# Experts of a decoder block: TensorE's instructions in the order of the program

## The chip, the cores and the metric

One Trainium2 chip, one of its cores. The core has five engines that run side by side and meet at semaphores: TensorE (PE in the profile, its weight loads as PEld), VectorE (DVE), ScalarE (ACT), GpSimd (POOL) and SyncE (SP), which here only issues DMA. Sixteen DMA engines move data between the memory (HBM) and the core's SBUF. The metric is the device time of one execution, in microseconds (us), as the median of several runs.

## The reference

One decoder block for 512 tokens of width 2048, all in float32. The first part is attention and retention with their projections; the change does not touch it. The second part is a mixture of 32 experts:

```python
g_sel = argmax(softmax(h @ w_rg + b_rg))             # one of 4 groups per token
top_p, top_i = top_k(softmax(e_logits of g_sel), 2)   # two of its 8 experts
weights = p_group * top_p / sum(top_p)
for e in range(32):                                   # D_MODEL 2048, D_EXPERT 512
    x_e = tokens that picked e
    y_e = (silu(x_e @ w1[e]) * (x_e @ w3[e])) @ w2[e]
out = rmsnorm(h + sum over picks of weight * y_e)
```

Each expert has w1, w3 (2048 x 512) and w2 (512 x 2048), 12.58 MB together; 32 experts have 402.7 MB. The 512 tokens make 1024 picks, 32 per expert in the mean.

## The kernel before

The kernel is written in a framework in which a scheduler decides, engine by engine, the order in which the traced instructions stand, from its own estimates of their durations. A function can take an engine out of its hands (`manual_schedule`): that engine's instructions then stand in the order in which the program wrote them. In the kernel before only SP is out of its hands, from the start on.

For each expert e the program traces these steps:

- **prep** (lines 714 to 755). GpSimd compares ranks and builds a selection matrix S (128 x 4 x 128, line 718). Four small matmuls (`ax`, line 723) give the inverse norms `rs` and, by way of three VectorE steps, the row numbers `idx` of the scatter. The gather (line 733) is 192 bf16 matmuls that pick up to 64 tokens out of the three bf16 parts of h, turned, in two halves g = 0 and 1 of 96 matmuls each, each in its own PSUM tile `gp`; VectorE scales each half into `xs` (line 736).
- **gemm1** (lines 762 to 780). `ab` = xs times w1 and w3: 16 steps, each of two float32 matmuls side by side in the two column halves of the array (line 759 in `halves_mm`). The two halves g of it use the weight tiles (0, 2) and (1, 3) of the expert. Then, in the same function, ScalarE copies `ab` out (line 772), TensorE turns it (`tr`, line 775), ScalarE takes the silu `sg` (line 777), VectorE multiplies to `gs` (line 779).
- **gemm2** (lines 785 to 815). `y` = gs times w2 in two halves q = 0 and 1; both halves read both of the expert's w2 tiles (4, 5). ScalarE copies half 0 and VectorE half 1 into `ysb`, and GpSimd issues an indirect DMA (line 813, the scatter) that writes the rows to `ybuf` in HBM. There is one `ysb`.

The outer loop (line 893 on) traces gemm1(e), prep(e + 1), gemm2(e - 1). The `y` and `ax` tiles share two PSUM buffers (`psY`).

Weights come in 192 loads of 2048 KB, six per expert, each into one of 8 buffers that are used in turn (`buffer`, `pieces_of`). SP issues them in the program's order: four for gemm1(e), then two for gemm2(e - 1). A load waits until the buffer that it takes, that of eight loads before, has been read for the last time, and the loads behind it in SP's queue wait with it. Near the end two of the eight buffers are kept for `fw` and `ys`. Behind the experts, `combine` (line 926) loads `ybuf` again, adds it to h, normalises and writes the output.

Of the kernel before, what the change touches and what calls it, by code (L numbers as in the profile page):

```python
# [11 lines left out]
F32 = mybir.dt.float32  # L12
F32R = mybir.dt.float32r
# [8 lines left out]
P = 128  # L22
D = 2048
# [6 lines left out]
NE = 32  # L30
# [96 lines left out]
def hybrid_block(ctx, tc, a, out):  # L127
    nc = tc.nc
# [303 lines left out]
    for j in range(KT):  # L432
        for n in range(2):
            acc = proj_T(f"g{n}", j)
            g = work("gs")
# [29 lines left out]
    with pool("mtmp", 2, reuse_waits="tile") as mt:  # L465
        for j in range(KT):
            hi, lo = unit("br", j, after=done[3] if j == 1 else None)
            gs, bs = [], []
            for n in range(2):
                g = mt.tile([P, T], F32, name=f"g{n}")  # L470
# [155 lines left out]
    scC = ExitStack()  # L626
# [28 lines left out]
    _, oh1 = first_max(LE, NT, NG, EPG)  # L655
    gm, ohg = first_max(L[:, :, :NG], NT, NG)
    nc.vector.scalar_tensor_tensor(LE2, oh1, NEG, LE, op0=OP.mult, op1=OP.add)
    _, oh2 = first_max(LE2, NT, NG, EPG)
# [43 lines left out]
    def buffer(shape=(P, 4096), dtype=F32, keep=False):  # L702

        pl, tag = next(x for x in loads if x[1] not in kept)
        if keep:
            kept.add(tag)
        return pl.tile(list(shape), dtype, name="wraw", tag=tag)

    gathering = []
    rowbase = rp[0].tile([P, 1], F32, name="rowbase")  # L710
    nc.gpsimd.memset(rowbase[:SLOTS], 8192.0)
# [2 lines left out]
    def prep(rsel, is2, eng, late=False):  # L714

        S = cp.tile([P, NT, P], BF, name="S")
        for t in range(NT):
            i = eng.tensor_scalar(S[:, t], slot1.rearrange("p a b -> p (a b)"), rsel[:, t:t + 1], None,  # L718
                                  op0=OP.is_equal)
        gathering.append(i.ins)  # L720
        ax = psY.tile([P, 40], F32, name="ax", tag="y")
        for t in range(NT):
            nc.tensor.matmul(ax, S[:, t], aux[:, t], start=(t == 0), stop=(t == NT - 1))  # L723
        rs = cp.tile([P, 1], F32, name="rs", bufs=3)
        nc.vector.reduce_sum(rs, ax[:, 0:3], axis=AX.X)
        xs = cp.tile([P, KT, SLOTS], F32, name="xs")
        for g in range(2):
            ks = slice(8 * g, 8 * g + 8)
            gp = psG.tile([P, 8, SLOTS], F32, name="gp")
            for d in range(8):  # L730
                for t in range(NT):
                    for i in range(3):
                        nc.tensor.matmul(gp[:, d], h3[i][:, t, (8 * g + d) * P:(8 * g + d + 1) * P],  # L733
                                         S[:, t, :SLOTS], start=(t == 0 and i == 0),
                                         stop=(t == NT - 1 and i == 2))
            nc.vector.tensor_mul(xs[:, ks], gp, b3(nfw[:, ks, None], 8, SLOTS))  # L736
        if late:
            ws = psY.tile([P, 3], F32, name="ws", tag="y")
            for t in range(NT):
                nc.tensor.matmul(ws, S[:, t], auxw[:, t], start=(t == 0), stop=(t == NT - 1))  # L740
            wsl = cp.tile([P, 1], F32, name="wsl", bufs=1)
            nc.vector.reduce_sum(wsl, ws, axis=AX.X)
            sp = psR.tile([P, NT, P], F32, name="tr")
            for t in range(NT):
                nc.tensor.matmul(sp[:, t], S[:, t], idb, start=True, stop=True)
            sT = cp.tile([P, NT, P], F32R, name="sT", bufs=1)
            nc.scalar.copy(sT, sp)
            return xs, rs, (wsl, sT)
        ix = cp.tile([P, 1], F32, name="ix", bufs=3)
        idx = cp.tile([P, 1], I32, name="idx", bufs=3)  # L750
        nc.vector.reduce_sum(ix, ax[:, 3:6], axis=AX.X)
        nc.vector.tensor_add(ix, ix, rowbase)
        nc.vector.scalar_tensor_tensor(idx, is2(ax[:, 8:40]), 2.0, ix, op0=OP.mult, op1=OP.add)
        return xs, rs, idx

    def halves_mm(acc, st, w, first, last):

        for m in range(2):
            nc.tensor.matmul(acc[m * SLOTS:(m + 1) * SLOTS], st, w[m], start=first, stop=last)  # L759

    def gemm1(blk, pieces):

        xs, rs, idx = blk
        acc = psA.tile([P, DE], F32, name="ab")
        for g in range(2):
            w = [next(pieces), next(pieces)]
            for kk in range(8):
                k = 8 * g + kk
                halves_mm(acc, xs[:, k], [w[m][:, kk * DE:(kk + 1) * DE] for m in range(2)],
                          k == 0, k == KT - 1)  # L770
        sb = cp.tile([P, DE], F32, name="ab", bufs=1)
        nc.scalar.activation(sb, acc, AF.Copy, scale=rs)  # L772
        tr = psR.tile([P, 4, P], F32, name="tr")
        for k in range(4):
            nc.tensor.transpose(tr[:, k], sb[:, k * P:(k + 1) * P], ident)
        sg = cp.tile([P, 4, SLOTS], F32, name="sg", bufs=1)
        nc.scalar.activation(sg, tr[:, :, :SLOTS], AF.Silu)
        gs = cp.tile([P, 4, SLOTS], F32, name="gs")
        last_ins.append(nc.vector.tensor_mul(gs, tr[:, :, SLOTS:], sg))
        return gs, idx  # L780

    last_ins = []
    yp = []

    def gemm2(blk, pieces, ys=None):

        gs, idx = blk
        if ys is not None:
            wsl, sT = idx
        else:  # L790
# [27 lines left out]
    def pieces_of(we, part):  # L818

        for q in ((4, 5) if part else (0, 2, 1, 3)):  # L820
            w = buffer()
            nc.sync.dma_start(w, we[q])
            yield w

    def prep_e(e):
        return prep(rank1[:, :, e], lambda c: c[:, e:e + 1], nc.gpsimd if e else nc.vector, e == NE - 1)
# [21 lines left out]
    def spread_fw(fw):  # L848

        for g in range(4):  # L850
            b = psR.tile([P, 4, P], F32, name="tr")
            for k in range(4):
                j = 4 * g + k
                nc.tensor.matmul(b[:, k], ident[:KT, j:j + 1].to_broadcast([KT, P]), fwk, start=True, stop=True)
            nc.scalar.copy(fw[:, g * T:(g + 1) * T], b.rearrange("p a b -> p (a b)"))
# [32 lines left out]
        return wt  # L888

    yp.append(scC.enter_context(pool("yout", 1, reuse_waits="tile")))  # L890
    x0 = prep_e(0)
    prev = None
    for e in range(NE):
        if e == NE - 1:
            fw = buffer((P, D), F32, True)
            ys = buffer((P, D), F32R, True)
            gemm2(prev, pieces_of(a["wM"][e - 1], 1))
            spread_fw(fw)
        cur = gemm1(x0, pieces_of(a["wM"][e], 0))
        if e == 8:  # L900
            with tc.issue_after(last_ins[-1].ins):
                nblk, eid, sta, en, it = extra_blocks()
        if e == 12:
            with tc.issue_after(last_ins[-1].ins):
                wtf = mixing()
        if e + 1 < NE:
            x0 = prep_e(e + 1)
        if 0 < e < NE - 1:
            gemm2(prev, pieces_of(a["wM"][e - 1], 1))
        prev = cur  # L910

    def diagonals():

# [3 lines left out]
        return dgs  # L917

    dgs = diagonals()
    sT = gemm2(prev, pieces_of(a["wM"][NE - 1], 1), ys)  # L920


    yv = ybuf.rearrange("(t p k) d -> t p k d", p=P, k=2)
# [48 lines left out]
    with tc.If(n_extra > 0):  # L972
        with tc.For_i(0, n_extra, 1):
# [11 lines left out]
            rsel, tmp4 = f("rsel", NT), oh1.rearrange("p t g j -> p t (g j)")  # L985
# [11 lines left out]
            ev = nc.values_load(eid[0:1, 0:1], engines=[mybir.EngineType.SP], min_val=0, max_val=NE - 1)  # L997

            we = a["wM"][ds(ev, 1)].rearrange("e q p n -> (e q) p n")
            gemm2(gemm1(prep(rsel, is2, nc.vector), pieces_of(we, 0)), pieces_of(we, 1))  # L1000
        combine(diagonals())
    scC.close()

# [69 lines left out]
```

## Time and profile before

| | us |
|---|---|
| median of 3 runs (2638.57 to 2646.08) | 2644.53 |
| the profiled execution, its own time | 2639.73 |
| its span, first to last instruction | 2637.9 |
| TensorE busy, of the span | 2433.3 |
| projections, attention, routing: up to about | 1440 |
| experts: from the first `ax` to the last `y` | 1442.7 to 2595.6 |
| the end (`combine`) | 2595.6 to 2637.9 |

The profile's page divides the span into 40 equal slices. Other views list the instructions in order of time, what each waited for, or the busy times of all engines in a chosen stretch. A busy PE says that matmuls were in its pipe, not that it ran at its best; PEclk is the share of full clock (2.4 GHz) that the chip granted.

### The profile page before, as it was taken

To read this page: it belongs to the slowest core of one execution; us is meant where nothing else is said; L and a number is where in the kernel's file an instruction comes from. 1 tells how busy PE (TensorE), PEld (TensorE's weight loads), DVE (VectorE), ACT (ScalarE), POOL (GpSimd) and SP (SyncE) were. 2 spreads that over 40 slices of the span, in tenths; PEclk is the share of its full clock that TensorE was granted. 3 is DMA by queue.
4 is the path that set the end of the run, shared out by engine and by line. 5 is a ranking of instruction groups with operands and counts; after the bars stand their busy time and mean duration, and the time that the engine had idled before them with its cause. 6 is when DMAs were issued, how large, how long until landed. Compare 5 with 4: busy or idle time off the path is not lost. (4 is left out here: it accounts for less than half of the span.)

```text
span 2637.9 us, 35885 instructions
## 1 busy us (share of the span) xinstructions
PE 2433.3 (92%) x16114; PEld 1625.7 (62%) x16114; DVE 716.1 (27%) x1269; ACT 468.4 (18%) x586; POOL 235.3 (9%) x330
## 2 busy tenths in 40 slices
PE   8999999999999999999998998899788877888887
PEld 7888888888888888888886453343333333333332
DVE  4444435534432222544234000010100000000005
ACT  5222223222222222322332000000000000000003
POOL 0000001101000000101113101111011101110002
PEclk9999999999999999999998999999999999999989
DMA  7233333222233333444326868898888789788896
GB/s 288 72 133 103 122 113 109 108 73 96 100 120 120 120 121 122 152 144 145 112 80 271 362 284 336 336 388 351 349 348 344 323 350 374 324 333 343 374 383 284
DMA packets 71438, 594.22 MB, mean 225 GB/s; under 512 B 8792, under 2 KB 25240, under 8 KB 37616
## 3 DMA queue, kind: packets, MB, share of 16 engines
q1 hardware_dynamic: 40320, 549.48, 51.7%
q0 software_dynamic: 9840, 25.61, 2.9%
q10 hardware_dynamic: 21120, 16.78, 1.9%
q8 instruction: 128, 2.10, 0.3%
q14 instruction: 30, 0.25, 0.0%
HBM read 562.72 MB, written 37.24 MB: 227 GB/s over the span
## 5 line engine op out<-in xcount | busy, mean ns | idle before, releaser
L759 PE MATMUL ab<-wraw,xs 128*64 128x512 f32 x2048 | 524.7, 636 | 113.8 <-DMA wraw<-in_wM_dram 113.8
L225 PE MATMUL acc<-xh,whl 128*128 128x512 f32 x1152 | 453.8, 394 | 0.0
L227 PE MATMUL acc<-xh,whl 128*128 128x512 f32 x1152 | 453.8, 394 | 0.0
L226 PE MATMUL acc<-xl,whl 128*128 128x512 f32 x1152 | 453.3, 393 | 0.0
L759 PEld LDWEIGHTS ab<-wraw,xs 128*64 128x64 f32 x2048 | 156.6, 146 | 430.5 <-issue 287.6
L96 ACT CAST whl<-wraw 128x2048 fp32r<-128x2048 f32 (+1 forms) x122 | 228.1, 1869 | 779.4 <-PE acc L227 412.4
L97 DVE TENSOR_TENSOR whl<-wraw,whl 128x2048 fp32r<-128x2048 f32 (+1 forms) x122 | 275.4, 2257 | 200.9 <-ACT whl L96 200.7
L736 DVE TENSOR_TENSOR xs<-gp,nfw 128x512 f32<-128x512 f32 x64 | 41.7, 687 | 792.4 <-PE ab L759 755.9
L759 PE MATMUL y<-wraw,gs 128*64 128x512 f32 x1024 | 244.7, 606 | 3.8 <-ACT ysb L802 1.2
L226 PEld LDWEIGHTS acc<-xl,whl 128*128 128x128 f32 x1152 | 216.6, 188 | 46.4 <-issue 1.4
L227 PEld LDWEIGHTS acc<-xh,whl 128*128 128x128 f32 x1152 | 216.6, 188 | 45.6 <-issue 1.4
L225 PEld LDWEIGHTS acc<-xh,whl 128*128 128x128 f32 x1152 | 216.6, 188 | 45.5 <-issue 0.5
L733 PEld LDWEIGHTS <-h 128*128 128x128 bf16 x6144 | 187.8, 98 | 60.2 <-issue 59.2
L733 PE MATMUL gp<-S,h 128*128 128x64 bf16 x6144 | 199.3, 194 | 25.2 <-POOL S L718 20.9
L772 ACT ACTIVATE ab<-ab,rs 128x512 f32<-128x512 f32 x32 | 22.0, 687 | 976.3 <-PE ab L759 957.2
L759 PEld LDWEIGHTS y<-wraw,gs 128*64 128x64 f32 x1024 | 77.0, 139 | 145.7 <-issue 112.6
L718 POOL TENSOR_SCALAR S<-slot,rank 128x128 bf16<-128x128 f32 x124 | 73.0, 599 | 897.7 <-PE ax L723 796.2
L242 PE MATMUL acc<-whl,xh 128*128 128x512 f32 x256 | 101.7, 401 | 6.7 <-ACT xh L201 6.7
L243 PE MATMUL acc<-whl,xh 128*128 128x512 f32 x256 | 102.7, 401 | 0.0
L595 PE MATMUL acc<-whl,mh 128*128 128x512 f32 x256 | 100.6, 393 | 0.0
L596 PE MATMUL acc<-whl,mh 128*128 128x512 f32 x256 | 100.4, 392 | 0.0
L479 PE MATMUL acc<-oh,whl 128*128 128x512 f32 x256 | 99.5, 390 | 0.6 <-DVE whl L85 0.6
(303 smaller groups left out, 2024.2 us busy)
## 6 DMA issues: line engine op xcount, KB each, us to landing
wraw<-in_wM_dram SPq DMA_DIRECT2D x192, 2048.0 KB, 18.5
wraw<-in_wA_dram SPq DMA_DIRECT2D x59, 2048.0 KB, 7.7
ybuf<-zero ACTq DMA_DIRECT2D x8, 1024.0 KB, 5.8
gate<-gs ACTq DMA_DIRECT2D x32, 256.0 KB, 2.0
g<-gate POOLq DMA_DIRECT2D x32, 256.0 KB, 3.0
wraw<-ybuf SPq DMA_DIRECT2D x4, 2048.0 KB, 15.1
xt<-in_x_dram SPq DMA_DIRECT2D x4, 1024.0 KB, 6.4
hc<-in_x_dram POOLq DMA_DIRECT2D x4, 1024.0 KB, 5.5
```

The costliest lines, as they stand in the source:

```text
L96: nc.scalar.copy(hi[:, c], w[:, c])
L97: nc.vector.tensor_sub(lo[:, c], w[:, c], hi[:, c].bitcast(F32))
L225: nc.tensor.matmul(acc, wh, xh[:, k], start=(k == 0), stop=False)
L226: nc.tensor.matmul(acc, wh, xl[:, k], start=False, stop=False)
L227: nc.tensor.matmul(acc, wl, xh[:, k], start=False, stop=(k == KT - 1))
L242: nc.tensor.matmul(accs[t], xh[:, k, s], wh, start=(k == 0), stop=False)
L243: nc.tensor.matmul(accs[t], xh[:, k, s], wl, start=False, stop=False)
L479: nc.tensor.matmul(b, wl, oh[i], start=False, stop=(k == H - 1))
L595: nc.tensor.matmul(accs[t], mh[k][:, s], wh, start=(k == 0), stop=False)
L596: nc.tensor.matmul(accs[t], mh[k][:, s], wl, start=False, stop=False)
L733: nc.tensor.matmul(gp[:, d], h3[i][:, t, (8 * g + d) * P:(8 * g + d + 1) * P], S[:, t, :SLOTS], start=(t == 0 and i == 0), stop=(t == NT - ...
L759: nc.tensor.matmul(acc[m * SLOTS:(m + 1) * SLOTS], st, w[m], start=first, stop=last)
```

## The change

TensorE is taken out of the scheduler's hands too, from the first prep on, and the program is written in the order in which its instructions are to stand:

- prep becomes a generator that stops after the first half of the gather and once more after the second;
- gemm1 ends with the copy of `ab` (line 772); what follows (transposes, silu, product) is a function of its own, `gated`;
- the loop traces gemm1(e); `ax` and gather half 0 of e + 1; the transposes of e; gather half 1 of e + 1; gemm2(e). For the first expert the second half of the gather stands between the halves of gemm1;
- gemm2(e) so comes one turn of the loop earlier, and with it its two loads in SP's queue: four for gemm1(e), two for gemm2(e);
- `spread_fw` (32 matmul instructions that spread the last norm's weights) moves from ahead of the last gemm1 to behind the last transposes.

The arithmetic, the tiles, the buffers and their number stay as they are.

```diff
+    scC.enter_context(tc.manual_schedule(engines={mybir.EngineType.SP, mybir.EngineType.PE}))
...
+        blk = [xs, rs, None]
         for g in range(2):
+            if g:
+                yield blk
...
-    def gemm1(blk, pieces):
+    def gemm1(blk, pieces, between=None):
...
             w = [next(pieces), next(pieces)]
+            if g and between is not None:
+                next(between)
...
         nc.scalar.activation(sb, acc, AF.Copy, scale=rs)
+        return sb
+
+    def gated(sb):
+
         tr = psR.tile([P, 4, P], F32, name="tr")
...
-    x0 = prep_e(0)
-    prev = None
+    nxt = prep_e(0)
+    cur = next(nxt)
     for e in range(NE):
-        if e == NE - 1:
-            fw = buffer((P, D), F32, True)
-            ys = buffer((P, D), F32R, True)
-            gemm2(prev, pieces_of(a["wM"][e - 1], 1))
-            spread_fw(fw)
-        cur = gemm1(x0, pieces_of(a["wM"][e], 0))
+        sb = gemm1(cur, pieces_of(a["wM"][e], 0), None if e else nxt)
...
+        was = cur
         if e + 1 < NE:
-            x0 = prep_e(e + 1)
-        if 0 < e < NE - 1:
-            gemm2(prev, pieces_of(a["wM"][e - 1], 1))
-        prev = cur
+            nxt = prep_e(e + 1)
+            cur = next(nxt)
+        gs = gated(sb)
+        if e + 1 < NE:
+            next(nxt)
+            if e == NE - 2:
+                fw = buffer((P, D), F32, True)
+                ys = buffer((P, D), F32R, True)
+            gemm2((gs, was), pieces_of(a["wM"][e], 1))
+    spread_fw(fw)
```

TensorE in the kernel before, between the gate products of experts 11 and 12. `tr_12667` is the turn of expert 11; `y_12611` with wraw_12597 is half q = 1 of gemm2(9); `y_12895` with wraw_12891 is half q = 0 of gemm2(10); `ab_12918` is gemm1(12); the gather `gp` there is for expert 14.

```order
L775 MATMUL tr_12667<-ident_73,ab_12665 128x128 x4
L759 MATMUL y_12611<-wraw_12597,gs_12086 64x512
L759 MATMUL y_12611<-wraw_12599,gs_12086 64x512
...
L723 MATMUL ax_12681<-aux_7849,S_12676 128x40
...
L733 MATMUL gp_13316<-S_13303,h3_0_7829 128x64
L759 MATMUL y_12895<-wraw_12891,gs_12380 64x512
L759 MATMUL y_12895<-wraw_12893,gs_12380 64x512
...
L759 MATMUL ab_12918<-wraw_12919,xs_12688 64x512
```

The scheduler took the two halves of a gemm2 apart: half 1 of gemm2(9) stands behind gemm1(11), and half 1 of gemm2(10) (`y_12905`) behind gemm1(12). The same place in the changed kernel, behind gemm1(11) (`ab_12654`); `ax_12702` and both `gp` are of expert 12, `tr_12808` of 11, `y_12925` and `y_12935` the two halves of gemm2(11), `ab_12948` gemm1(12):

```order
L766 MATMUL ab_12654<-wraw_12677,xs_12415 64x512
L724 LDWEIGHTS S_12697
L724 MATMUL ax_12702<-aux_7849,S_12697 128x40
...
L737 MATMUL gp_12710<-S_12697,h3_2_7831 128x64
L788 MATMUL tr_12808<-ident_73,ab_12695 128x128 x4
...
L737 MATMUL gp_12817<-S_12697,h3_2_7831 128x64
L766 MATMUL y_12925<-wraw_12921,gs_12815 64x512
...
L766 MATMUL y_12935<-wraw_12923,gs_12815 64x512
L766 MATMUL ab_12948<-wraw_12949,xs_12709 64x512
```

Both halves of gemm2(11) now stand ahead of gemm1(12), so w2 of an expert is read for the last time one gemm1 and more earlier. SP's queue in the kernel before, from the loads for gemm2(9) (wraw_12597, 12599) on; then four for gemm1(11), two for gemm2(10), four for gemm1(12), two for gemm2(11). The bracket names the semaphores that a load waits for, PE for TensorE, DMAHW for an earlier load:

```order
L822 DMA wraw_12597<-in_wM_dram 128x4096 [waits DMAHW2_49,PE_49]
...
L822 DMA wraw_12891<-in_wM_dram 128x4096 [waits DMAHW0_49]
L822 DMA wraw_12893<-in_wM_dram 128x4096 [waits DMAHW1_49]
L822 DMA wraw_12919<-in_wM_dram 128x4096 [waits DMAHW2_49,PE_49]
L822 DMA wraw_12921<-in_wM_dram 128x4096 [waits DMAHW3_49,PE_49]
L822 DMA wraw_12939<-in_wM_dram 128x4096 [waits DMAHW4_49]
L822 DMA wraw_12941<-in_wM_dram 128x4096 [waits DMAHW5_49]
L822 DMA wraw_13224<-in_wM_dram 128x4096 [waits DMAHW6_49]
L822 DMA wraw_13226<-in_wM_dram 128x4096 [waits DMAHW7_49]
```

The load of wraw_12919 takes the buffer of wraw_12597, eight loads before, whose last reader is `y_12611`; the loads behind it need readers that stood ahead of that one on TensorE, and no wait of their own. In the changed kernel, with w2 of expert 11 (wraw_12921, 12923), then the four of gemm1(12) and the two of gemm2(12):

```order
L835 DMA wraw_12921<-in_wM_dram 128x4096 [waits DMAHW2_49,PE_49]
L835 DMA wraw_12923<-in_wM_dram 128x4096 [waits DMAHW3_49,PE_49]
L835 DMA wraw_12949<-in_wM_dram 128x4096 [waits DMAHW4_49,PE_49]
L835 DMA wraw_12951<-in_wM_dram 128x4096 [waits DMAHW5_49,PE_49]
L835 DMA wraw_12969<-in_wM_dram 128x4096 [waits DMAHW6_49,PE_49]
L835 DMA wraw_12971<-in_wM_dram 128x4096 [waits DMAHW7_49,PE_49]
L835 DMA wraw_13254<-in_wM_dram 128x4096 [waits DMAHW0_49,PE_49]
L835 DMA wraw_13256<-in_wM_dram 128x4096 [waits DMAHW1_49,PE_49]
```

Every load now waits for a matmul of its own: the pair for gemm1(12)'s first half takes the buffers of gemm2(10), the second pair those of gemm1(11)'s first half, the pair for gemm2(12) those of gemm1(11)'s second half.

## Rows read from the trace of the kernel before

**Rows 1.** The page, 40 slices of the span: granted clock, DMA rate.

```profile
PEclk9999999999999999999998999999999999999989
GB/s 288 72 133 103 122 113 109 108 73 96 100 120 120 120 121 122 152 144 145 112 80 271 362 284 336 336 388 351 349 348 344 323 350 374 324 333 343 374 383 284
```

**Rows 2.** Stretches: us, busy of PE, PEld, DVE, ACT, POOL, PEclk, DMA share, GB/s.

```profile
1460.00:2600.00 1140.00, 973.39 (x9292) 433.03 (x9289) 96.60 (x296) 61.92 (x113) 102.38 (x151) 0.96 0.85 351
2600.00:2638.00 38.00, 20.12 (x71) 9.29 (x69) 29.30 (x80) 16.54 (x40) 10.10 (x8) 0.85 0.51 204
```

**Rows 3.** ACT in order of time, start and us: first and last `ab` copy of 32.

```profile
1463.79 0.69 ACT L772 ACTIVATE ab<-ab,rs 128x512 f32<-128x512 f32 x1 [28.53 <-PE ab L759]
...
2586.13 0.69 ACT L772 ACTIVATE ab<-ab,rs 128x512 f32<-128x512 f32 x1 [10.43 <-PE ab L759]
```

**Rows 4.** PE and PEld in order of time, one turn; brackets: idle before, releaser.

```profile
2021.86 0.66 PE L775 MATMUL tr<-ident,ab 128*128 128x128 f32 x4 [0.83 <-ACT ab L772]
2022.57 3.65 PE L759 MATMUL y<-wraw,gs 128*64 128x512 f32 x16
2026.16 0.17 PEld L723 LDWEIGHTS <-S 128*128 128x128 bf16 x4 [0.81 <-issue]
2026.16 0.27 PE L723 MATMUL ax<-aux,S 128*128 128x40 bf16 x4
2027.39 3.65 PE L759 MATMUL y<-wraw,gs 128*64 128x512 f32 x16
2030.98 3.24 PE L733 MATMUL gp<-S,h 128*128 128x64 bf16 x105
2035.15 2.68 PE L733 MATMUL gp<-S,h 128*128 128x64 bf16 x86
2039.94 7.09 PE L759 MATMUL ab<-wraw,xs 128*64 128x512 f32 x32 [2.11 <-DMA wraw<-in_wM_dram]
2050.54 9.97 PE L759 MATMUL ab<-wraw,xs 128*64 128x512 f32 x30 [3.51 <-DMA wraw<-in_wM_dram]
2061.34 0.66 PE L775 MATMUL tr<-ident,ab 128*128 128x128 f32 x4 [0.83 <-ACT ab L772]
```

**Rows 5.** SP's DMA queue in order of time, 2021 to 2061.

```profile
2026.22 2.99 SPq L822 DMA_DIRECT2D wraw<-in_wM_dram  x6
```

**Rows 6.** DMA from 2021 to 2061, 40 slices of 1 us: busy tenths, GB/s.

```profile
DMA  4100009589999989799899998997998998997100
GB/s 180 66 0 0 0 0 262 197 344 492 426 393 459 430 352 528 311 492 459 360 492 426 393 475 377 426 492 328 459 492 344 475 475 360 475 410 328 49 16 0
```

**Rows 7.** Waits in total: us, times, longest.

```profile
SPq L822 <- PE ax L723: 852.0, 27, 36.9
...
PE ab L759 <- DMA wraw<-in_wM_dram: 113.8, 57, 3.6
```

**Rows 8.** Stretches without a pause of the DMA, columns as in rows 2.

```profile
2516.00:2584.00 68.00, 59.08 (x259) 21.27 (x257) 2.89 (x7) 5.55 (x10) 2.87 (x3) 0.90 1.01 427
...
1459.00:1498.00 39.00, 38.50 (x515) 21.36 (x513) 4.71 (x14) 4.01 (x6) 4.66 (x8) 1.00 1.00 419
1742.00:1799.00 57.00, 56.23 (x558) 25.15 (x556) 4.03 (x11) 2.93 (x5) 3.37 (x5) 0.97 1.00 421
```

**Rows 9.** The page's group of `xs`: busy us, mean ns, idle before.

```profile
L736 DVE TENSOR_TENSOR xs<-gp,nfw 128x512 f32<-128x512 f32 x64 | 41.7, 687 | 792.4 <-PE ab L759 755.9
```

**Rows 10.** DMA issues: the scatter, median us from issue to landing.

```profile
ybuf<-ysb,idx POOLq DMA_INDIRECT x31, 11.4
```

**Rows 11.** PE in order of time: gemm1(0).

```profile
1449.71 13.96 PE L759 MATMUL ab<-wraw,xs 128*64 128x512 f32 x64
```

**Rows 12.** PE in order of time: `spread_fw` in two parts, last gemm2.

```profile
2549.69 2.31 PE L854 MATMUL tr<-fwk,ident 16*128 16x128 f32 x16 [0.73 <-ACT sT L747]
...
2560.32 2.05 PE L854 MATMUL tr<-fwk,ident 16*128 16x128 f32 x16
...
2588.46 7.14 PE L759 MATMUL y<-wraw,gs 128*64 128x512 f32 x32 [0.28 <-DVE gs L779]
```

More of the change, by code (lines that the diff above doesn't have):

```diff
@@ L747, in prep @@
             nc.scalar.copy(sT, sp)
-            return xs, rs, (wsl, sT)
+            blk[2] = wsl, sT
+            yield blk
+            return
         ix = cp.tile([P, 1], F32, name="ix", bufs=3)
@@ L753, in prep @@
         nc.vector.scalar_tensor_tensor(idx, is2(ax[:, 8:40]), 2.0, ix, op0=OP.mult, op1=OP.add)
-        return xs, rs, idx
+        blk[2] = idx
+        yield blk
     def halves_mm(acc, st, w, first, last):
@@ L759, in halves_mm @@
             nc.tensor.matmul(acc[m * SLOTS:(m + 1) * SLOTS], st, w[m], start=first, stop=last)
-    def gemm1(blk, pieces):
-        xs, rs, idx = blk
+    def gemm1(blk, pieces, between=None):
+        xs, rs, _ = blk
         acc = psA.tile([P, DE], F32, name="ab")
@@ L779, in gemm1 @@
         last_ins.append(nc.vector.tensor_mul(gs, tr[:, :, SLOTS:], sg))
-        return gs, idx
+        return gs
     last_ins = []
@@ L785, in gemm2 @@
     def gemm2(blk, pieces, ys=None):
-        gs, idx = blk
+        gs, (_, _, idx) = blk
         if ys is not None:
@@ L919, in hybrid_block @@
     dgs = diagonals()
-    sT = gemm2(prev, pieces_of(a["wM"][NE - 1], 1), ys)
+    sT = gemm2((gs, was), pieces_of(a["wM"][NE - 1], 1), ys)
     yv = ybuf.rearrange("(t p k) d -> t p k d", p=P, k=2)
@@ L999, in hybrid_block @@
             we = a["wM"][ds(ev, 1)].rearrange("e q p n -> (e q) p n")
-            gemm2(gemm1(prep(rsel, is2, nc.vector), pieces_of(we, 0)), pieces_of(we, 1))
+            *_, blk = prep(rsel, is2, nc.vector)
+            gemm2((gated(gemm1(blk, pieces_of(we, 0))), blk), pieces_of(we, 1))
         combine(diagonals())
```

## The prediction

> **What bounds the kernel now.** I read the 40 slices of the page first [rows 1]: but for the first slice, up to about 1385 us the DMA moves 70 to 152 GB/s; from there on, with few exceptions, 320 to 390. So the experts are a stage of their own, in which the weights count. The stage in one line [rows 2]: over 1140 us the DMA engines are busy for 0.85 of the time and move 351 GB/s, TensorE is busy for 973 us of the 1140. Neither is full, so the two take turns in waiting. The `ab` copies give the pace: 32 of them, from 1463.79 to 2586.13 [rows 3], so (2586.13 - 1463.79) / 31 = 36.2 us per expert.
>
> Why both wait is read from one turn in order of time [rows 4]. The transposes start at 2021.86, half 1 of an older expert's gemm2 at 2022.57, half 0 of a younger one's at 2027.39, the gather runs until about 2038, and then TensorE waits 2.11 us and, in the middle of gemm1, 3.51 us for weights. All six loads of the turn leave SP's queue at 2026.22, within 2.99 us [rows 5], when the half at 2022.57 is done. The DMA shows the other side [rows 6]: four slices with nothing moved ahead of 2027, then some 30 us at 330 to 530 GB/s, then little again after 2058. It is a ring: the late half of gemm2 frees one pair of buffers, everything behind it in SP's queue leaves at once, TensorE works off what it holds (one w2 and gathers), waits for the first pair until 2039.94, for the second until 2050.54, and only then comes to the next late half. That this holds for nearly every turn is in the waits [rows 7]: SP's loads wait 27 times, 852 us in all, to about the moment at which `ax` starts, and `ab` waits 57 times for weights, 113.8 us.
>
> **The change, part by part.**
>
> *The release of buffers.* In the new order the loads are freed pair by pair, by gemm1's two halves and by gemm2, each pair as soon as its expert has used it. With four pairs of buffers, three per expert, TensorE works on one while up to three are landing or queued. The six loads of a turn that left together now leave in three pairs some 7 to 14 us apart, and the DMA always has work queued once it is the slower side. So its price per expert is bytes over rate: 6 x 2.097 MB plus a scatter of about 0.26 MB (1024 picks x 8 KB / 32) = 12.85 MB. The rate when the DMA does not pause is seen in three stretches [rows 8]: 427 GB/s over 68 us, 419 over 39, 421 over 57. With 12.85 MB that is 30.1 to 30.7 us; I take 423 GB/s, 30.4.
>
> The Trainium skill, page "DMA: Bandwidth & Descriptors", section "Specifications", gives an HBM limit of about 358 GB/s per core and says under "Where 436 GB/s comes from" that this side binds for HBM to SBUF; by that an expert would cost 35.9 us and the change would bring next to nothing. The 427 GB/s over 68 us speak against that limit here (the same page has 425 for one large transfer with the other core idle); it stays as a rival below.
>
> *TensorE's own time.* All 192 gather matmuls, `ax`, the transposes and the products stay; only their order changes. Per expert: two halves of gemm1 at 7.09 us, two of gemm2 at 3.65, a gather of 3.24 + 2.68 (191 of 192 instructions), 0.27 for `ax`, 0.66 for the transposes [rows 4] = 28.3 us. Changes between float32 and bf16 work: there are four per turn, and one costs up to the 0.81 us that the load for `ax` sat idle at such a place [rows 4]; most of that lies under the modelled end of the matmuls ahead (2022.57 + 3.65 = 2026.22, and `ax` starts at 2026.16). So 28.3 to 31.5 us, and I take 29, since the rows that follow each other start within 0.1 us of the modelled end. That is under 30.4: TensorE waits some 1.4 us per expert, and the DMA becomes the bound.
>
> *New waits in the fixed order.* The copy of `ab` (0.69 us [rows 3]) is hidden by a half gather of 3 us; silu, product and `xs` of half 0 (0.69 [rows 9]) by the other half; `xs` of half 1 by gemm2, 7.3 us. If that cover were gone, some 2 us per expert. `ax` waits for the PSUM buffer of gemm2's half 0 of two experts ago, whose copy needs the scatter before it to have landed (11.4 us from issue [rows 10]), and behind `ax` the whole of TensorE is queued. The copy, the scatter's issue and the landing take some 14 us after a gemm2, and the next gemm2 comes 20 us after it: nothing.
>
> *The queues.* On SP, w2 of e moves ahead of w13 of e + 1: same bytes, same count. GpSimd has scatter(e) ahead of S(e + 2), 2.4 us of compares that `ax` needs a whole gemm1 later. Nothing.
>
> *The start.* gemm1(0) now has half of gather 0 between its halves, so it starts 3 us earlier, 1446.7 for 1449.71 [rows 11]; its first half is done at 1453.8 and the first waiting pair leaves. Eight loads are in by then. In the first experts TensorE is the slower side with uneven steps; I follow the pairs for ten experts with the durations above and find some 5 us in which the DMA idles.
>
> *The end.* `spread_fw` (2.31 + 2.05 us [rows 12]) now stands between the last transposes and the last gemm2, where it hides 1.7 us of silu and product: +2.7 us. `combine` is VectorE's, busy 29.3 of the last 38 us [rows 2]; the fixed order of its matmuls costs 0 to 3 us, I take 1.
>
> **The sum.** From load 8 on 184 x 2.097 = 385.9 MB of weights and 8.1 MB of scatters, 394.0 MB, at 423 GB/s 931.5 us. Start 1455 (1453.8 and about 1 us of way), gaps 5: the last pair lands at 2391.5. The pair before it, gemm1(31)'s second, lands 9.9 earlier, at 2381.6; half a gemm1 7.1, copy and transposes 1.4, `spread_fw` 4.4, then gemm2 7.3: the last `y` ends at 2401.8. In the trace it ends at 2588.46 + 7.14 = 2595.6 [rows 12]. That is 193.8 us less, minus 1 for `combine`: 2639.73 - 192.8 = 2447 for the profiled execution, whose own time lies 4.8 under the median of 2644.53. **Forecast 2452 us**, 7.3% faster.
>
> **The rivals.**
>
> *TensorE becomes the bound.* With 31.5 us per turn (each change of type exposed, or the hiding above not complete) it no longer waits for weights. gemm1(31) then starts at 1446.7 + 31 x 31.5 = 2423.2, the last `y` ends 27.3 us later (14.2 + 1.4 + 4.4 + 7.3), at 2450.5, 145 us sooner than now: 2500. For it: the fixed order cannot fill a gap with other work, and 29 is only 1.4 under the DMA. Against: the rows above follow each other without gaps.
>
> *The memory does not keep the rate.* If 351 GB/s, the mean of the whole stage [rows 2], is what the memory gives in the long run, and the 427 a burst after a rest, 394.0 MB take 1122.5 us and the last `y` ends at 2593: 2643, no change. Against: 68 us without pause is two experts long [rows 8]. (The skill's page named above is the rule of this rival; at its 358 GB/s it would be 2621.)
>
> *Slower: the clock falls.* Where TensorE had waited 3.51 us, the next half took 9.97 us for 7.09 [rows 4]: 2.9 us more, as of 5.8 us at half of full clock, the lower level of 1.2 GHz. If the new order's waits, one per expert and at the same place, put both halves of every gemm1 at that level, a turn costs 29 + 14.2 = 43.2, and 31 turns 217 us more than now: 2860. It decides from 36.2 on, that is with 14 us of every turn at the lower level. Against: the waits shrink from 2.1 + 3.5 us per turn to about 1.4, a wait of 2.11 us left the next half at 7.09 [rows 4], and the stretches with TensorE at its fullest show a clock of 0.97 to 1.00 [rows 8]. A slow half also eats up the wait that caused it.
>
> That the change does not do what it says is no rival: the order of both queues shows it.
>
> **How the numbers follow.** Forecast (2430 to 2480) 0.73; TensorE as the bound (2480 to 2530) 0.15; the memory's rate (2600 to 2650) 0.05; the clock (over 2652) 0.03; the rest 0.04 on either side. The low end of the range: 427 GB/s (9 us) and no early gaps (5) and a shorter end, 2430; the high end takes in the rival with TensorE as the bound and leaves out the other two: 2520. Faster by over 0.3% (8 us, about what can be told from no change) 0.92, within it 0.04, slower 0.04.
>
> **What would show it.** In the profile after: `ab` copies 30 to 31 us apart; the DMA share at 0.98 or more and some 420 GB/s over the stage; loads leaving in pairs; SP's waits going to `ab` and `y`, not to `ax`; one wait of `ab` or `y` for weights per expert, of 1 to 2 us; clock at 0.97 or more; the last `y` near 2402. If TensorE is the bound, there are no waits for weights and the DMA share is about 0.95. If the memory is, the DMA share is full at 350 to 360 GB/s. If VectorE or ScalarE holds TensorE, `tr` or `y` shows it as waits for `ab` or `gs`. The prediction is wrong at its root if SP's loads still leave six at a time.

## The result and the profile after

The kernel after takes 2459.14 us in the median (2456.61 to 2459.81, 4 runs). The kernel before, measured beside it, takes 2641.55 us (2635.15 to 2646.08, 4 runs). The ratio is 0.9309, with a 95% interval of 0.9286 to 0.9332. The profiled execution after took 2456.61 us, its span is 2454.9 us, 183.0 less than before.

The page of the kernel after, 40 slices of the span (granted clock, DMA rate), the lines that answer to [rows 1]:

```profile
PEclk9999999999999999999999989999999999999998
GB/s 290 98 107 126 110 98 142 78 112 73 108 78 129 129 124 105 116 157 150 150 109 102 137 306 404 426 425 426 425 426 426 425 426 423 424 426 424 426 398 219
```

From the 26th slice to the 38th the DMA rate is a flat line at 423 to 426 GB/s, where before it moved between 320 and 390. Four stretches of the same stage, for [rows 2] and [rows 8] (us, busy time of PE, PEld, DVE, ACT, POOL, then PEclk, DMA share, GB/s):

```profile
1460.00:1500.00 40.00, 39.01 (x500) 20.38 (x497) 4.71 (x14) 4.01 (x6) 4.56 (x7) 1.00 0.94 381
1500.00:2340.00 840.00, 789.89 (x8236) 375.97 (x8236) 91.57 (x267) 49.20 (x88) 95.16 (x140) 0.99 1.01 425
2340.00:2400.00 60.00, 55.03 (x505) 24.94 (x502) 5.04 (x11) 4.38 (x9) 3.11 (x4) 1.00 0.95 391
2412.00:2455.00 43.00, 24.19 (x85) 10.47 (x84) 32.62 (x82) 18.46 (x44) 11.28 (x8) 0.83 0.34 137
```

For 840 us the DMA never pauses (share 1.01) and the clock is granted at 0.99. The first and the last of the 32 `ab` copies, for [rows 3]:

```profile
1466.65 0.69 ACT L781 ACTIVATE ab<-ab,rs 128x512 f32<-128x512 f32 x1 [31.57 <-PE ab L766]
...
2397.25 0.69 ACT L781 ACTIVATE ab<-ab,rs 128x512 f32<-128x512 f32 x1 [19.98 <-PE ab L766]
```

(2397.25 - 1466.65) / 31 = 30.0 us per expert for 36.2. That is where the time went. From first to last copy it is 930.6 us for 1122.3, 191.7 less; the first copy comes 2.9 later; from the last copy to the end of the span it is 57.7 us for 51.8, 5.9 more: 191.7 - 2.9 - 5.9 = 182.9 of the 183.0.

One turn of TensorE in order of time, for [rows 4]:

```profile
2032.53 0.27 PE L724 MATMUL ax<-aux,S 128*128 128x40 bf16 x4
2032.64 2.96 PE L737 MATMUL gp<-S,h 128*128 128x64 bf16 x96
2035.44 0.63 PE L788 MATMUL tr<-ident,ab 128*128 128x128 f32 x4
2035.91 2.90 PE L737 MATMUL gp<-S,h 128*128 128x64 bf16 x94
2040.00 0.22 PE L737 MATMUL gp<-S,h 128*128 128x64 bf16 x2 [1.18 <-issue]
2040.14 7.09 PE L766 MATMUL y<-wraw,gs 128*64 128x512 f32 x32
2047.06 13.90 PE L766 MATMUL ab<-wraw,xs 128*64 128x512 f32 x64
```

Both halves of a gemm2 stand together, the transposes no longer wait for the copy of `ab`, and in this turn no product waits for weights. It is one of the shorter turns, 28.4 us from `ax` to the next `ax` at 2060.90; the turn ahead of it took 33.4. Six loads in a row that left ahead of it, from SP's queue in three stretches of time (start, us in the queue's issue, count), for [rows 5]:

```profile
2012.55 0.80 SPq L835 DMA_DIRECT2D wraw<-in_wM_dram  x2
...
2019.72 1.17 SPq L835 DMA_DIRECT2D wraw<-in_wM_dram  x2
...
2031.78 1.17 SPq L835 DMA_DIRECT2D wraw<-in_wM_dram  x2
```

Three pairs, 7.2 and 12.1 us apart, instead of six loads within 2.99 us. The waits in total (us, times, longest), for [rows 7]:

```profile
SPq L835 <- PE y L766: 418.6, 31, 17.0
SPq L835 <- PE ab L766: 396.2, 58, 30.6
...
PE ab L766 <- DMA wraw<-in_wM_dram: 38.9, 21, 3.6
PE gp L737 <- issue: 16.1, 12, 1.7
```

SP now waits for the gate products (`ab`, gemm1's products with w1 and w3) and for `y`, and for the moment of `ax` only 61.7 us in 30 waits. The gate products wait for weights 21 times, 38.9 us for 113.8. This looks like the DMA as the bound, with TensorE waiting for it now and then; e4 and e5 below put it to the test.

### The profile page after: what moved, and what is told of

Read it like the earlier page. It is cut to its first block, busy times and chain, and to the rows that moved or that the text cites. A ratio compares the mean times of both kernels' runs of the same rounds, so it can differ in the third digit from the quotient of the medians.

```text
span 2454.9 us, 36000 instructions
## 1 busy us (share of the span) xinstructions
PE 2357.7 (96%) x16112; PEld 1618.9 (66%) x16114; DVE 725.4 (30%) x1269; ACT 471.3 (19%) x586; POOL 237.1 (10%) x330
## 5 line engine op out<-in xcount | busy, mean ns | idle before, releaser
L766 PE MATMUL ab<-wraw,xs 128*64 128x512 f32 x2048 | 480.2, 602 | 40.6 <-DMA wraw<-in_wM_dram 38.9
L766 PE MATMUL y<-wraw,gs 128*64 128x512 f32 x1024 | 229.1, 599 | 0.0
L737 PE MATMUL gp<-S,h 128*128 128x64 bf16 x6144 | 193.1, 193 | 16.1 <-issue 16.1
L737 PEld LDWEIGHTS <-h 128*128 128x128 bf16 x6144 | 187.9, 98 | 18.4 <-issue 18.1
L766 PEld LDWEIGHTS y<-wraw,gs 128*64 128x64 f32 x1024 | 71.1, 137 | 131.6 <-issue 129.9
L726 DVE TENSOR_REDUCE rs<-ax 128x1 f32<-128x3 f32 x32 | 5.1, 160 | 459.1 <-PE ax L724 459.1
```

## The experiments

Theory: the loads left six at a time because half 1 of each gemm2 stood one gemm1 late; with both halves together the buffers come free pair by pair, the DMA never pauses, and its rate sets the time. The rivals: the fixed order of TensorE as such, or the hiding (copy of `ab`, silu and product, `xs` behind half gathers and gemm2). All times are medians; each ratio is against the kernel before, run beside it.

| kernel | us | ratio, 95% interval | us per expert |
|---|---|---|---|
| e1_fixed_alone | 2457.92 | 0.9327, 0.9312 to 0.9343 | 30.2 |
| e2_no_hiding | 2479.22 | 0.9415, 0.9393 to 0.9437 | 30.65 |
| e3_program_order | 2477.74 | 0.9400, 0.9384 to 0.9416 | 30.8 |
| e6_late_half | 2599.91 | 0.9857, 0.9840 to 0.9875 | 34.5 |
| e4_fewer_bytes | 2387.47 | 0.9048, 0.9022 to 0.9074 | 27.7 |
| e5_less_tensor | 2454.89 | 0.9304, 0.9278 to 0.9330 | 30.0 |
| e9_fewer_bytes_bare | 2486.90 | 0.9428, 0.9401 to 0.9455 | 30.9 |

### The release of buffers: e1 and e6

e1 is the old program with one line more:

```diff
+    scC.enter_context(tc.manual_schedule(engines={mybir.EngineType.SP, mybir.EngineType.PE}))
     gathering = []
```

> The kernel before with the line that fixes TensorE's order and nothing else: the old program (gemm1(e), transposes, whole gather of e + 1, gemm2(e - 1)), so both halves of a gemm2 stand together, nothing hides the copy of ab. Theory (what counts is that w2's buffers come free in one piece, so that the loads leave in pairs): the DMA is full, experts 30 to 31 us apart, 2455 to 2480 us. Rival 1 (the new order of the program counts, with its hiding and its earlier gemm2): 2560 to 2640. Loads in SP's queue leave in twos under the theory, in sixes under rival 1.

Measured 2457.92 us, no slower than the whole change. The stretch 1500 to 2300, columns as above, and one turn of TensorE:

```profile
1500.00:2300.00 800.00, 739.01 (x7773) 352.12 (x7770) 82.77 (x253) 46.79 (x83) 89.51 (x131) 1.00 1.00 423
```

```profile
2024.67 0.65 PE L776 MATMUL tr<-ident,ab 128*128 128x128 f32 x4 [0.83 <-ACT ab L773]
2025.17 0.26 PE L724 MATMUL ax<-aux,S 128*128 128x40 bf16 x4
2025.27 5.76 PE L734 MATMUL gp<-S,h 128*128 128x64 bf16 x192
2030.96 7.09 PE L760 MATMUL y<-wraw,gs 128*64 128x512 f32 x32
```

The transposes wait 0.83 us for the copy, as before the change, and the gather is not split. Yet the DMA is full at 423 GB/s, since `y` stands in one piece: around this turn the loads leave SP's queue two at a time, at 2023.04, 2038.07 and 2044.94. So neither the generator, nor the split gather, nor the earlier gemm2 was needed for the gain.

e6 is the kernel after, in which half 1 of gemm2(e) alone is moved behind gemm1(e + 1):

```diff
         for q in range(2):
+            if q and ys is None:
+                yield
             y = psY.tile([P, DE], F32, name="y")
...
         sb = gemm1(cur, pieces_of(a["wM"][e], 0), None if e else nxt)
+        if late is not None:
+            next(late)
...
-            gemm2((gs, was), pieces_of(a["wM"][e], 1))
+            late = gemm2((gs, was), pieces_of(a["wM"][e], 1))
+            next(late)
```

> The kernel after, its order fixed as there, but half 1 of gemm2(e) stands behind gemm1(e + 1) instead of next to half 0, as in the kernel before. The same instructions, one group of 8 products moved per turn. Theory: w2's pair of buffers comes free behind gemm1(e + 1), three pairs of loads leave at once, TensorE waits for the first two of them with nothing else to do; with 13.7 and 24.3 us from release to landing as in rows 4 and 5 a turn is 35 to 38 us, 2590 to 2660 us, and the loads leave in sixes. Rival (a fixed order with the hiding is what brought the gain): 2459 to 2480 us.

Measured 2599.91 us: 140.8 of the 182.4 us are lost again by one moved half. TensorE from the end of one late half to the next one, and the DMA in the turn ahead of it, 40 slices from 2006.5 to 2041 (busy tenths, GB/s):

```profile
2037.45 4.02 PE L766 MATMUL y<-wraw,gs 128*64 128x512 f32 x15
2041.40 0.27 PE L724 MATMUL ax<-aux,S 128*128 128x40 bf16 x4
...
2049.47 3.65 PE L766 MATMUL y<-wraw,gs 128*64 128x512 f32 x16
...
2055.04 7.09 PE L766 MATMUL ab<-wraw,xs 128*64 128x512 f32 x32 [1.07 <-DMA wraw<-in_wM_dram]
2064.86 6.65 PE L766 MATMUL ab<-wraw,xs 128*64 128x512 f32 x29 [2.73 <-DMA wraw<-in_wM_dram]
...
2075.30 0.27 PE L724 MATMUL ax<-aux,S 128*128 128x40 bf16 x4
```

```profile
DMA  0948999999998989999998999989999898997100
GB/s 0 285 133 361 418 399 475 370 423 408 442 465 380 475 361 456 437 418 456 418 456 361 437 475 399 456 380 475 418 437 456 380 475 380 437 475 323 57 38 0
```

This is the ring of [rows 4] and [rows 6] again: the DMA stops at the end of a turn, starts with the release, and TensorE waits for the first and for the second pair, until 13.6 and 23.4 us behind the end of the late half (2037.45 + 4.02 = 2041.47). This turn takes 2075.30 - 2041.40 = 33.9 us. Over all turns e6 stays 1.7 us per expert under the kernel before (34.5 for 36.2), and this is not the ring: from 1500 to 2300 us TensorE is busy for 676 us in e6 and 683 before, which makes 29.1 and 30.9 us per expert, so that its idle time is 5.3 us per expert in both. The granted clock of that stretch is 0.98 in e6 and 0.96 before, a part of the difference; the rest of it is not broken down. The theory stands; the strict order on TensorE as such is not the cause.

### The order of the program without a fixed order: e3

The kernel after without its line for TensorE; the scheduler arranges the new program. In its order the halves of gemm2 stay together.

```diff
-    scC.enter_context(tc.manual_schedule(engines={mybir.EngineType.SP, mybir.EngineType.PE}))
```

> The kernel after without the line that fixes TensorE's order: the program is written in the new order, the scheduler arranges TensorE's instructions. In its order both halves of a gemm2 stay together and the first gate product of the next expert stands ahead of most of a gather. Theory (release in one piece counts): 2450 to 2485 us with a full DMA. Rival (it is the strict order on TensorE that counts): back toward the kernel before, 2560 to 2640.

Measured 2477.74 us, within what the theory gave, but 18.6 us above the kernel after. Products wait for weights only once in it, 2.5 us: TensorE is the bound, at 30.8 us per expert. A part of one turn shows what lengthens it:

```profile
2037.19 0.47 PE L736 MATMUL gp<-S,h 128*128 128x64 bf16 x10
2037.59 1.07 PE L765 MATMUL ab<-wraw,xs 128*64 128x512 f32 x2
2038.59 2.89 PE L736 MATMUL gp<-S,h 128*128 128x64 bf16 x93
2041.41 7.08 PE L765 MATMUL ab<-wraw,xs 128*64 128x512 f32 x30
```

The gather is cut into pieces between gate products, and two gate products alone hold TensorE for 1.0 us (2037.59 to 2038.59), where 30 in a run take 7.0, 0.47 for two. The copy of `ab` is not covered either: `tr` waits for it 29 times, 25.0 us. The two make 1.4 us, where 3.8 stand between 27.0 (the plain turn of the kernel after) and 30.8; other turns are cut more often, and the rest is not broken down. The one line and the new program each put gemm2 together; the line also keeps the pieces whole.

### What bounds the kernel after: e5 and e4

e5 leaves the third part of h out of the gather, 2 us of TensorE per turn; the output lacks that part.

```diff
-                    for i in range(3):
+                    for i in range(2):
```

> The kernel after with two of the three parts of h in the gather, 128 products for 192 per expert, 2 us less of TensorE's time per turn (the output loses the third part). Theory (DMA is the bound): the waits of the gate products for weights grow by about 2 us per turn and the time stays, 2450 to 2461 us. Rival (TensorE is the bound): 31 x 2 = 62 us less, about 2397.

Measured 2454.89 us, 4 less than after and not 62; the ratios, 0.9304 and 0.9309, do not tell the two apart. The waits for weights in total:

```profile
PE ab L766 <- DMA wraw<-in_wM_dram: 79.2, 37, 4.0
```

79.2 us for 38.9: of the 62 us that TensorE was spared, 40 are waits now. The granted clock over 1500 to 2300 us fell to 0.96 from 0.99, so that some of the rest went into slower products. The first turns, which do not yet wait, fell from 27.0 to 25.2 us.

e4 loads half of each w2 tile; half 1 of gemm2 uses the columns of half 0 again, so the work on TensorE is the same.

```diff
-                ws = slice((4 * q + k) * DE, (4 * q + k + 1) * DE)
+                ws = slice(k * DE, (k + 1) * DE)
...
-            nc.sync.dma_start(w, we[q])
+            nc.sync.dma_start(w[:, :2048] if part else w, we[q][:, :2048] if part else we[q])
```

> The kernel after with half of each w2 tile loaded; gemm2's half 1 multiplies with the columns of half 0 again, so the instructions on TensorE are the same and the output is not the reference's. Bytes per expert 12.85 - 2.10 = 10.75 MB, 25.4 us at 423 GB/s. Theory (after is bound by the DMA, TensorE's own turn is 27.0 us, as in its first experts): TensorE becomes the bound, 27.0 to 27.6 us per expert, no waits for weights, 31 x (30.0 - 27.3) = 84 us less, 2365 to 2385 us. Rival (after is bound by TensorE or by a chain of waits): 2445 to 2460.

Measured 2387.47 us, 2.5 above the upper end that I gave, and far from the rival's 2445. The same stretch:

```profile
1500.00:2300.00 800.00, 785.22 (x8512) 376.53 (x8512) 93.75 (x271) 50.75 (x90) 96.33 (x141) 1.00 0.94 386
```

The DMA has room (0.94), TensorE is busy for 785 of 800 us, and no product waits for weights. Experts are 27.7 us apart: 27.0 in the plain turns and 1 to 2 more where the gather has a gap (below). Less work for TensorE brings next to nothing, fewer bytes bring 72 us: the DMA is the bound.

### What the hiding is worth: e2 and e9

e2 is the kernel after in the plainest order: gemm1, transposes, gemm2, then the whole prep of e + 1.

```diff
         was = cur
-        if e + 1 < NE:
-            nxt = prep_e(e + 1)
-            cur = next(nxt)
         gs = gated(sb)
         if e + 1 < NE:
-            next(nxt)
...
             gemm2((gs, was), pieces_of(a["wM"][e], 1))
+            nxt = prep_e(e + 1)
+            cur = next(nxt)
+            next(nxt)
```

> The kernel after with nothing hidden: gemm1(e), transposes, gemm2(e), then ax and the whole gather of e + 1. TensorE waits for the copy of ab (about 0.8 us), for silu and product (about 1.7) and for xs (about 0.7) in each turn, 3.2 us more on TensorE. Theory (the DMA is the bound, 30.0 us per expert where TensorE alone needs 27.0): the waits for weights shrink instead, 2455 to 2485 us. Rival (TensorE's own time is on the path and the hiding pays in full): 31 x 3.2 = 99 us more than 2459, so 2540 to 2560.

Measured 2479.22 us, 20 more than after, 79 less than a full payment would have made it. One turn:

```profile
1853.01 13.95 PE L766 MATMUL ab<-wraw,xs 128*64 128x512 f32 x64
1867.83 0.66 PE L788 MATMUL tr<-ident,ab 128*128 128x128 f32 x4 [0.86 <-ACT ab L781]
1869.48 7.09 PE L766 MATMUL y<-wraw,gs 128*64 128x512 f32 x32 [0.99 <-DVE gs L792]
1876.50 0.27 PE L724 MATMUL ax<-aux,S 128*128 128x40 bf16 x4
1876.62 5.76 PE L737 MATMUL gp<-S,h 128*128 128x64 bf16 x192
1882.31 3.22 PE L766 MATMUL ab<-wraw,xs 128*64 128x512 f32 x14
```

The two idle times of 0.86 and 0.99 us are there, 29.3 us per turn (1853.01 to 1882.31) for 27.0. On top come gaps in the gather, 11 times and 17.3 us in all, and 9 gemm2 of 8.7 to 8.8 us for 7.09. The mean is 30.65, just over the DMA's 30.0. No product waits for weights any more, and though the DMA is full too (423 GB/s from 1500 to 2300), e9 below shows that fewer bytes do not help: TensorE has become the bound, and only the part above the DMA's pace is paid.

e9 is e2 and e4 together, to see the hiding where the DMA is not the bound:

> e2 and e4 together: half of each w2 tile loaded and nothing hidden (gemm1, transposes, gemm2, whole gather). In e2 experts were 29.3 us apart, with a gap of about 1.6 us in the gather in every second one. Theory (e2 is bound by TensorE already): fewer bytes bring it little, 30.0 to 30.6 us per expert, 2455 to 2480 us; against e4 the hiding is then worth 2.3 to 3 us per expert, 70 to 100 us, where the DMA is not the bound. If the gaps in the gather come from the full DMA and go with it: 29.3 us per expert, 2435 to 2445.

Measured 2486.90 us, 7 above the range that I gave. Against e4 the hiding is worth 99 us, 3.2 per expert (30.93 for 27.68), of which a plain turn of 29.4 for 27.0 explains 2.4. Part of the rest goes with the clock: of the 31 gemm2 ahead of the last, 10 took more than 7.3 us in e9 (some 1.7 us more than the 7.09 of the others) and 2 in e4; this makes about half of the rest, and what else is in it stays open. One of the ten started at 2026.85, behind the two idle times, and took 8.78 at a granted clock of 0.81, a mix of the two levels of 1.2 and 2.4 GHz. That e9 stands 7.7 us above e2, with fewer bytes, is no difference shown: the two ran on different chips, the kernel before beside e9 was itself 4.9 us slower, and the intervals of the two ratios overlap. The gaps in the gather did not go with the full DMA (10 times, 15.9 us, at a DMA share of 0.88), so that cause for them falls.

### The end: e8, and e10 to e13

e8 puts `spread_fw` behind gemm2(30):

```diff
             gemm2((gs, was), pieces_of(a["wM"][e], 1))
-    spread_fw(fw)
+            if e == NE - 2:
+                spread_fw(fw)
```

> The kernel after with spread_fw behind gemm2(30) instead of behind the last transposes. There TensorE works 4.0 us before gemm1(31), which waited 2.3 us for its second pair of weights anyway; behind the last transposes 1.5 us of silu and product come to light. Theory: of the 4.0 us on the path 2.5 go, less up to 1.7 by which gemm1(31) comes later: 2455 to 2458 us. Rival (the end hangs on w2's last pair, which lands at about 2398, and on the loads of ybuf, at about 2410): no change, 2459.

Measured 2454.18 us, 0.8 under the range that I gave, ratio 0.9299 (0.9273 to 0.9325). Since 5 us lie near what can be told, after and e8 were run again side by side:

> The kernel after, unchanged, beside e11 on the same chip: 2457 to 2461 us, for the comparison of a difference of 0.2%.

> The kernel of e8 (spread_fw behind gemm2(30)) again. Theory: the 5 us between the 2454.18 of e8 and the 2459.14 of after are real, so here 3 to 6 us under e10. Rival: they lie between two chips or two sets of runs, so within 2 us of e10.

Measured 2460.59 (2456.93 to 2464.77, ratio 0.9345, 0.9318 to 0.9371) and 2457.03 us (2451.42 to 2458.38, ratio 0.9330, 0.9305 to 0.9355): 3.6 us, in the direction and of the size of the theory, with runs that overlap. The end on TensorE in e11:

```profile
2379.49 3.88 PE L867 MATMUL tr<-fwk,ident 16*128 16x128 f32 x32
2383.29 13.95 PE L766 MATMUL ab<-wraw,xs 128*64 128x512 f32 x64
...
2399.70 7.09 PE L766 MATMUL y<-wraw,gs 128*64 128x512 f32 x32 [0.93 <-DVE gs L792]
```

`spread_fw` takes the place of the wait for gemm1(31)'s second pair, and the last gemm2 starts at 2399.70, 2.8 us before that of the kernel after.

e12 takes the buffers of `fw` and `ys` later; e13 is e12 with e8:

```diff
-            if e == NE - 2:
-                fw = buffer((P, D), F32, True)
-                ys = buffer((P, D), F32R, True)
             gemm2((gs, was), pieces_of(a["wM"][e], 1))
+            if e == NE - 2:
+                fw = raw2.tile([P, D], F32, name="wraw", tag="r3")
+                ys = raw2.tile([P, D], F32R, name="wraw", tag="r2")
+                kept.update(("r2", "r3"))
```

> The kernel after, but fw and ys take their two buffers behind gemm2(30) (those that w2 of expert 30 had) instead of ahead of its loads. In after only three pairs are left for the last loads, and from 2346 to 2352 the DMA moves 200 to 260 GB/s; over 2340 to 2400 it moves 391 GB/s for 425 before, 60 x 34 / 425 = 4.8 us. Theory: with four pairs to the end this dip goes, the last two pairs land 4 to 5 us sooner, 2454 to 2457 us. Rival (the dip has another cause, or the loads of ybuf, which now wait for gemm1(31)'s second half, take the gain back): 2457 to 2461, no change.

> e12 and e8 together: the two buffers taken behind gemm2(30), and spread_fw there too. Theory (both gains lie on the same path, the last weights, then gemm1(31), gemm2(31)): 3.6 us of e11 and 4 of e12, 2449 to 2454 us, the fastest. Rival (VectorE's work on ybuf's loads ends last, whatever TensorE does): 2456 to 2459.

Measured 2457.42 us (ratio 0.9330, 0.9307 to 0.9352) and 2454.47 us (0.9319, 0.9296 to 0.9342). The DMA from 2340 to 2400 in 40 slices of 1.5 us, first in the kernel after, then in e12:

```profile
GB/s 393 360 393 328 262 229 218 197 339 371 404 388 445 407 464 388 470 382 470 393 470 382 492 360 492 382 470 404 415 448 385 440 407 478 393 448 273 350 404 448
```

```profile
GB/s 437 404 448 415 437 426 404 448 350 448 415 448 421 448 415 426 437 393 448 415 426 437 404 426 437 437 404 459 371 382 358 279 287 229 218 240 371 426 437 437
```

The dip at 2346 to 2352 is gone and has come back at 2386 to 2394: the weights are through sooner, and the DMA then waits for the loads of `ybuf`, which leave at 2392.43 (2392.53 in the kernel after). So the buffers were the cause of the dip, but no time comes of it: gemm1(31)'s second half still waits 2.29 us for its pair and starts at 2389.86, for 2390.08 in the kernel after. The rival holds for e12. e13 falls between the two ranges that I gave for it; it is 3.0 us under e12, as e11 is 3.6 under e10. Both differences point the way of the theory of e8, but the runs overlap, and so do the ratios of e8, e11, e13 and the kernel after: no version here is shown to be better than the change.

## Why the prediction was right, by its steps

The time, 2459.14 for 2452, lies in the range, and the case is the one forecast: DMA as the bound. The profiled execution came 9.6 us above its forecast (2456.61 for 2447), and the step from it to the median was 2.5 us for the 4.8 that I took, so that 7.1 remain.

**The release.** Right, and shown as the cause by e1 and e6: loads leave in pairs, and one half of gemm2 moved back brings the ring back.

**The rate.** I took 423 GB/s from three stretches of 39 to 68 us; it is 425 over 840 us. That the memory would not keep the rate was the rival behind the 2643; it is out. By the 358 GB/s that the page "DMA: Bandwidth & Descriptors" of the Trainium skill, section "Specifications", gives as the limit of a core this could not be; the page "Perfetto Trace Analysis" of the Trainium skill, section "Roofline", says that a single core whose partner is idle can pull more than that, up to some 435 GB/s of its DMA engines. The trace agrees with the second, at 425 GB/s; every run here used one core.

**TensorE's turn.** Mis-sized: 29 us, from a sum of 28.3, where the plain turns and e4 show 27.0. The rows' durations overlap: gemm2's 7.09 us row is followed 6.92 later (2040.14 to 2047.06), the 2.96 of half a gather 2.80 later. Added up by starts, the rows of a plain turn give 27.0. This had no weight for the time, since the DMA is slower either way, but it made the rival with TensorE as the bound look nearer than it was; 0.15 was too much for it. The waits for weights came to 38.9 us, 1.25 per expert, for 1.4, and that they agree is luck: TensorE had 3.0 us per expert to spare (30.0 less 27.0), not 1.4. Of the 3.0, 1.25 are recorded as waits and 0.5 as gaps in the gather; in the other 1.2 products took longer than in a plain turn, such as 8.71 us for 7.08 behind a wait:

```profile
2023.88 8.71 PE L766 MATMUL ab<-wraw,xs 128*64 128x512 f32 x30 [3.34 <-DMA wraw<-in_wM_dram]
```

**The new waits.** Right: in all 32 turns the waits of `tr`, `ax` and the gate products for another engine are one of 0.8 us, one of 0.8, and two of 0.8, and `y` has none. Their cover is worth less than the 2 us per expert that I named for its loss: e2 lost 20 us, 0.6 per expert. Where the DMA is not the bound, from e4 to e9, it is worth 3.2.

**The start.** gemm1(0) began at 1448.66, not 1446.7: the first half gather took 4.61 us for 2.96, at a granted clock of 0.61 from 1443 to 1448, and `xs` held gemm1 for 0.79. The clock there was in no term of mine.

**The end.** The last `y` ended at 2402.49 + 8.78 = 2411.3, forecast 2401.8. This is the 9.5 us by which the sum is short, and the end on TensorE shows its parts:

```profile
2379.86 7.89 PE L766 MATMUL ab<-wraw,xs 128*64 128x512 f32 x34
2390.08 7.08 PE L766 MATMUL ab<-wraw,xs 128*64 128x512 f32 x30 [2.33 <-DMA wraw<-in_wM_dram]
2397.99 0.66 PE L788 MATMUL tr<-ident,ab 128*128 128x128 f32 x4 [0.83 <-ACT ab L781]
2398.57 3.98 PE L867 MATMUL tr<-fwk,ident 16*128 16x128 f32 x32
2402.49 8.78 PE L766 MATMUL y<-wraw,gs 128*64 128x512 f32 x32
```

gemm1(31)'s second half ended at 2397.2 for 2388.7: 8.5 us. Two terms were mis-sized, the gaps and the spacing of the last pairs. Against 425 GB/s the stretch 1460 to 1500 lost 40 x 44 / 425 = 4.1 us, 1455 to 1460 (216 GB/s) 2.5 and 2340 to 2400 4.8, 11.4 for the 5 that I had, all of which I had put at the start; the higher rate gave 4.4 back (394.0 MB at 425 for 423 GB/s), so 2.0 of the 8.5 are left to the gaps. Overlap did the rest: the last two pairs share the rate, so the second to last lands not 9.9 but some 7 us before the last (I put the landing of the last at about 2398, 17.3 us behind its issue at 2380.05, the median there), and the loads of `ybuf` run beside it from 2392.53 on. What each of these two is worth is an estimate and was not tested by a run. Copy, transposes and `spread_fw` took 5.3 us for 5.8, the last gemm2 8.78 for 7.3. Its own stretch shows why:

```profile
2402.50:2411.30 8.80, 8.77 (x33) 2.70 (x34) 1.29 (x2) 3.09 (x5) 0.00 (x0) 0.81 1.00 428
```

A clock of 0.81 was granted there, part of the stretch at the lower level of 1.2 GHz, behind the waits of 2.33 and 0.83 us and `spread_fw`. In e11 the same gemm2, with no such wait ahead of gemm1's second half, took 7.09 at 1.00.

**The tail.** From the end of the last `y` to the end of the span it is 43.6 us for 42.3, 1.3 more for the 1 that I took.

**The slower rival.** The clock did not fall: 0.99. e5 shows its pieces in small: with 2.5 us of waits per turn the granted clock from 1500 to 2300 is 0.96, and some products are slower, while the time stays.

## What to carry to other kernels

In a ring of buffers the reader that stands last sets the time at which everything behind it in the load queue may leave: look which instruction a queue waits for, and whether a scheduler has put half of a consumer far behind the other half. A load queue that empties in one burst while the DMA idles for part of every turn is the sign; what is left once the loads no longer bunch is bytes over the rate in a stretch without a pause. Once the DMA is full, hidden waits on the other engines are worth only what exceeds its pace, as e1 and e2 show, with e9 beside them; time an engine's turn by the starts of its rows, not by the sum of their durations.

## What the runs showed of the hardware that I had not expected

A gather of 192 short products has gaps of its own. In the kernel after it idles 12 times, 16.1 us in all, up to 1.7 each, with nothing that the profile shows to wait for (`PE gp L737 <- issue` above, and the 1.18 us at 2040.00). With 192 products in a row it is 15 times in e1, 11 in e2 and 10 in e9; with 96 and 96 it is 12 in the kernel after and in e4, 13 in e6; in e5, with 64 and 64, no such wait appears. In e4 and e9 the DMA share between 1500 and 2300 us is 0.94 and 0.88, so the gaps do not need a full DMA, and an unbroken run of 192 has not clearly more of them than two of 96.

The traces say more. In all these runs the gaps stand behind 129 to 191 products of a gather; e5's gather has 128. In the kernel after and in e1 they follow each other at 893, 638 or 255 of TensorE's matmuls, with 27 to 92 us between them. And the profile has a DMA queue for instructions, on the page of the kernel after

```profile
q8 instruction: 128, 2.10, 0.3%
```

that is 128 packets of 16 KB. In each of the 12 gaps of the kernel after such a packet starts 0.7 to 1.5 us before the gap, and the products go on 2.3 to 2.6 us behind its start. At 2040.00 the packet starts at 2037.6, the gap at 2038.8. So the gaps go with the loading of instructions; that the loading holds TensorE up is the likely reading, and no run changed it to see.

The DMA of one core moved 425 GB/s for 840 us, and 426 for 800 us in e5, nearly all of it weights read from the memory.
